# A decoder layer on one core: two more products by quarters, seven instead of eight

## The chip, the cores and the metric

The kernel runs on one NeuronCore of a Trainium2 chip. The metric is the device time of one execution in microseconds; the time before is the median of three runs. A profile is one execution recorded by the hardware profiler. Engines are named as it names them: PE is the matrix engine (PEld its weight loads), DVE the vector engine, ACT the scalar engine, POOL the GpSimd engine, SP the engine that issues most DMAs.

## The reference

One decoder layer on x of 512 tokens and 1024 channels, float32:

```python
h = x @ w_in[i]
ua, va, za, qh, kh, vh, zb, ga, gb = jnp.split(h, IN_OFFSETS, axis=-1)
...
ya = ua * sa.reshape(bn, s_len, A_WIDTH) * jax.nn.silu(za)
...
yb = o.reshape(bn, s_len, B_WIDTH) * jax.nn.silu(zb)
merged = jax.nn.sigmoid(ga) * (ya @ w_branch_a[i]) + jax.nn.sigmoid(gb) * (yb @ w_branch_b[i])
mix_out = merged @ w_out[i]
ple = jax.nn.sigmoid(x @ w_ple_gate[i]) * (p[i] @ w_ple[i])
x = layer_norm(DEEPNORM_ALPHA * x + mix_out + ple, ln_g[i], ln_b[i])
```

Branch A is gated spatial mixing, branch B differential attention. What matters here is the last part: the products `ya @ w_branch_a` (called `wa` in the kernel), `yb @ w_branch_b` (`wb`), `merged @ w_out` (`out`), each 512 x 1024 by 1024 x 1024, and the last norm.

## The kernel before

**Numbers.** PE multiplies rounded halves. Every float32 operand is split into a high part (a copy rounded to float32r, by ACT) and a low part (the rest, a subtraction by DVE), and `three` (L282) issues three products per tile: high by high, high by low, low by high. `cut` does this for activations; for weights `prep` and `spread` do, on tiles of 128x1024 that a DMA brought (`wr`, split into `wh` and `wl`; L400 the copy, L403 the subtraction).

**Order.** The program is written out in one order. `product` (L270) counts PE's products on a clock and runs an agenda: `later(n, fn)` puts a step n products further on. The instructions of each engine stand in the order in which the agenda emits them, each engine works its own queue in that order, and semaphores make it wait for others. An engine's instruction whose operand is late holds up all behind it.

**Two ways to multiply.** `token_chunk` takes a stage in two column halves; each of its 8 weight tiles serves all 4 token tiles, 24 products. `quad` takes the 512 x 1024 operand in quarters (two halves of the tokens, two of the inner channels) and does seven products of quarters instead of eight, 24 products in each of seven steps. It needs sums of quarters on both sides. The sums of the weights are made by DMAs that add to what lies in a tile (`follow`, L375, on POOL's queue) or ready in DRAM; those of activations must be there as further operands (`operands`, L635). The seven results are combined from the PSUM banks: ACT keeps some in SBUF (`keep`, L651), DVE adds or subtracts (`block`, L656), and `done` takes the result on. Two weight tiles serve only 24 products then, and are split one step ahead.

**Stages.** v, va, za, ga, gb, pg and `wb` use `quad`; `wa` and `out` use `token_chunk`, and the last four token tiles of `out`'s second half are written out, the last in two halves of 256 columns. Between, `ple` multiplies the embeddings. ga and gb wait in DRAM and come back as tiles. `mb_done` (L1325) multiplies `wb`'s result by its gate, `merge` (L1348, L1349) multiplies `wa`'s and adds, `merge_turn` transposes the merged tile on PE and splits it, `residue` (L1280) adds alpha x to the embeddings in `base`, `residual` (L1375) adds `out`'s bank and takes the statistics, `last_norm` (L1382, L1386) finishes a token tile and stores it. All of these run on DVE, except the transposes and a power of the variance on POOL (L1181).

## Time and profile before

| what | us |
|---|---|
| median of three runs | 620.74 |
| lowest and highest | 620.26, 621.10 |
| the profiled execution: its span (all that the page gives of its time) | 618.3 |
| of it DVE busy | 458.8 |
| of it ACT busy | 327.3 |
| PE's last product ends, from the span's start | 611.3 |

The span runs from the first to the last instruction. The page names a tile written and the tiles read (`out<-in`), how many, the busy time and the mean of one. A busy time adds up stretches in which at least one instruction ran; matmuls overlap, so their own durations (0.39 us) are longer than the distance of their starts. A row of the timeline gives the start, the duration, the engine, the line and the operation; in brackets stands the idle time of the engine before it and what ended it.

### The profile page before, as it was taken

To read this page: it belongs to the slowest core of one execution; us is meant where nothing else is said; L and a number is where in the kernel's file an instruction comes from. 1 tells how busy PE (TensorE), PEld (TensorE's weight loads), DVE (VectorE), ACT (ScalarE), POOL (GpSimd) and SP (SyncE) were. 2 spreads that over 40 slices of the span, in tenths; PEclk is the share of its full clock that TensorE was granted. 3 is DMA by queue.
4 is the path that set the end of the run, shared out by engine and by line. 5 is a ranking of instruction groups with operands and counts; after the bars stand their busy time and mean duration, and the time that the engine had idled before them with its cause. 6 is when DMAs were issued, how large, how long until landed. Compare 5 with 4: busy or idle time off the path is not lost.

```text
span 618.3 us, 8634 instructions
## 1 busy us (share of the span) xinstructions
PE 610.0 (99%) x3036; PEld 514.3 (83%) x3036; DVE 458.8 (74%) x800; ACT 327.3 (53%) x528; POOL 108.7 (18%) x120
## 2 busy tenths in 40 slices
PE   9999999999999999999999999999999999999995
PEld 6888888888888888888889988888888888888885
DVE  6996587878878866857578887677657659476486
ACT  6655664655645655478656765456567445232200
POOL 1234021332432620230102120111110010000011
PEclk9999999999999999999999999999999999999999
DMA  8689899679798598689898898999978997753002
GB/s 305 220 244 183 263 301 271 230 206 283 250 268 282 182 281 267 156 271 304 272 308 197 228 247 242 223 249 284 270 207 259 354 270 241 235 193 117 1 34 103
DMA packets 49888, 143.78 MB, mean 233 GB/s; under 512 B 6452, under 2 KB 7604, under 8 KB 49524
## 3 DMA queue, kind: packets, MB, share of 16 engines
q1 hardware_dynamic: 38772, 110.05, 50.4%
q0 software_dynamic: 8192, 28.58, 25.7%
q10 hardware_dynamic: 2880, 4.59, 2.0%
q8 instruction: 24, 0.39, 0.3%
q14 instruction: 20, 0.16, 0.1%
HBM read 120.00 MB, written 34.73 MB: 250 GB/s over the span
## 4 chain that ended last, share of the span: by engine, by line
PE 99%; DVE 0%; issue 0%; DVEq 0%
PE ps_pp L271 56%; PE ps_sc L271 18%; PE ps_tx L271 9%; PE ps_sc L821 3%; PE ps_po L866 3%; PE ps_po L271 3%; PE ps_tr L271 3%; PE ps_tr L855 1%; PE ps_po L475 1%; PE ps_tr L1208 1%; PE ps_po L1208 1%; PE ps_tx L905 0%; PE ps_sc L1355 0%; PE ps_pp L1355 0%; DVE base L1386 0%
## 5 line engine op out<-in xcount | busy, mean ns | idle before, releaser
L403 DVE TENSOR_TENSOR wl<-wr,wh 128x1024 fp32r<-128x1024 f32 (+1 forms) x136 | 166.4, 1227 | 53.8 <-ACT wh L400 53.1
L400 ACT ACTIVATE wh<-wr 128x1024 fp32r<-128x1024 f32 (+1 forms) x136 | 139.9, 1033 | 87.1 <-PE ps_po L271 15.6
L271 PE MATMUL ps_pp<-xh,wh 128*128 128x512 f32 (+1 forms) x276 | 109.5, 397 | 0.0
L271 PE MATMUL ps_pp<-xl,wh 128*128 128x512 f32 (+1 forms) x276 | 107.0, 388 | 0.0
L271 PE MATMUL ps_pp<-xh,wl 128*128 128x512 f32 (+1 forms) x276 | 105.4, 382 | 0.0
L834 ACT ACTIVATE p<-p,sth 128x128 f32<-128x128 f32 (+3 forms) x64 | 35.5, 556 | 47.3 <-DVE sth L832 47.2
L271 PEld LDWEIGHTS ps_pp<-xh,wl 128*128 128x128 f32 x276 | 52.0, 189 | 8.7
L271 PEld LDWEIGHTS ps_pp<-xh,wh 128*128 128x128 f32 x276 | 52.2, 189 | 8.4 <-ACT wh L297 0.5
L271 PEld LDWEIGHTS ps_pp<-xl,wh 128*128 128x128 f32 x276 | 52.2, 189 | 8.3 <-DVE xl L298 0.4
L375 POOL DMA_DIRECT2D wr<-in_w x26 | 22.6, 869 | 156.8 <-DVE wl L403 136.8
L828 DVE CUSTOM_DVE_ANT_0 p<-ps_sc,mask 128x128 f32<-128x128 f32 (+3 forms) x64 | 30.9, 483 | 5.6 <-PE ps_sc L821 5.6
L766 POOL TENSOR_TENSOR hl<-m,hl 128x512 fp32r<-128x512 f32 x16 | 25.1, 1609 | 54.7 <-ACT hl L761 54.7
L271 PE MATMUL ps_pp<-wh,xl 128*128 128x512 f32 x84 | 32.9, 391 | 0.0
L271 PE MATMUL ps_pp<-wl,xh 128*128 128x512 f32 x84 | 32.8, 390 | 0.0
L271 PE MATMUL ps_pp<-wh,xh 128*128 128x512 f32 x84 | 32.7, 389 | 0.0
L271 PE MATMUL ps_sc<-wh,xsh 128*128 128x512 f32 x80 | 31.2, 390 | 0.0
L271 PE MATMUL ps_sc<-wl,xsh 128*128 128x512 f32 x80 | 31.1, 389 | 0.0
L271 PE MATMUL ps_sc<-wh,xsl 128*128 128x512 f32 x80 | 31.1, 389 | 0.0
L1181 POOL TENSOR_TENSOR rs<-mv,mhalf 128x1 f32<-128x1 f32 x8 | 7.7, 961 | 121.6 <-DVE mv L1179 121.6
L271 PE MATMUL ps_pp<-wl,xsh 128*128 128x512 f32 x64 | 25.0, 391 | 0.0
L271 PE MATMUL ps_pp<-wh,xsl 128*128 128x512 f32 x64 | 25.0, 391 | 0.0
L271 PE MATMUL ps_pp<-wh,xsh 128*128 128x512 f32 x64 | 25.0, 390 | 0.0
(365 smaller groups left out, 1389.7 us busy)
## 6 DMA issues: line engine op xcount, KB each, us to landing
wr<-in_w SPq DMA_DIRECT2D x83, 512.0 KB, 4.7
wr<-in_w POOLq DMA_DIRECT2D x22, 512.0 KB, 6.1
k<-hl SPq DMA_DIRECT2D x16, 256.0 KB, 5.2
q<-hl SPq DMA_DIRECT2D x16, 256.0 KB, 4.3
ws_va<-in_w POOLq DMA_DIRECT2D x8, 512.0 KB, 10.9
wr<-ws_va SPq DMA_DIRECT2D x8, 512.0 KB, 4.3
wa<-in_w POOLq DMA_DIRECT2D x6, 512.0 KB, 7.3
kx<-hl SPq DMA_DIRECT2D x12, 256.0 KB, 5.8
```

Of the source, the lines that this page charges most:

```text
L271: pe.matmul(ps, s, m, start=start, stop=stop, skip_group_check=read_within)
L375: pool.dma_start(out=raw[u][:, :n], in_=weights(STEPS[FOLLOWS[u]][1], n), accum_op=OP.add)
L400: act.activation(h, raw[u][:, :width(STEPS[u][0])], AF.Copy)
L403: dve.tensor_tensor(out=l, in0=raw[u][:, :width(STEPS[u][0])], in1=h.bitcast(F32), op=OP.subtract)
L475: pe.matmul(idle, zeros[:, :P], zeros, start=True, stop=True)
L766: pool.tensor_tensor(out=hl[:, 3 - j, :], in0=m[2 * j], in1=hl[:, j, :].bitcast(F32), op=OP.subtract)
L821: pe.matmul(sc[m][:, :n], q[:, m, i * P:(i + 1) * P], kk[:, m, :n], start=o == 0, stop=o == 1)
L828: dve.tensor_tensor_reduce(out=pr[m][:, :n], in0=sc[m][:, :n], in1=mask[:, T - n:], scale=-(DK ** -0.5), scalar=3e38, op0=OP.add, op1=OP.m ...
L834: act.activation(pr[m][:, :n], pr[m][:, :n], AF.Exp, bias=st[:, m:m + 1], scale=-1.0, accum_out=st[:, 2 + m:3 + m])
L866: pe.matmul(po[:, i * P:(i + 1) * P], at[:, j * P:(j + 1) * P], v[:, j, h * P:(h + 1) * P], start=j == 0, stop=j == i)
L1181: pool.tensor_tensor(out=rs, in0=mv[:, 1:2], in1=mhalf[:, 0:1], op=OP.pow)
L1208: pe.matmul(sa[:, t * P:(t + 1) * P], va[:, t, g * P:(g + 1) * P], aux[0][:, 0, g, :], start=True, stop=True)
```

## The change

`wa` and `out` become `quad`s (`add` becomes `quad` in `plan`). What they need is added and moved:

- yb's operands (three parts, and four sums read from DRAM) go into the tiles of x's parts, and are issued during `pg`; ya's parts and sums are issued from `ple` on, during `wb`. The sums of ya are made by POOL, in place of ya's quarters.
- The gates of `wb` (six of eight), the residues and the merges (six of eight) move from DVE to POOL; ACT multiplies x by alpha.
- The merged result is transposed; ACT copies it into the place of ua, DVE takes its sums partly straight from the transposed banks, POOL makes two of the differences.
- `out` is added onto `base` piece by piece: ACT's kept banks by POOL, the others by DVE at times that `FOLD` sets.
- The norm of the first two token tiles is divided among ACT, DVE and POOL (`early_norm`); the other two stay with `last_norm`. The seventh step's second token tile is done in two halves of 256 columns.

```diff
+CUTS_YA = (((4, 7), (1, 1), 1, 1), ((76, 7), (0, 0), 0, 0), ((100, 7), (1, 0), 1, 0),
+           ((124, 7), 0, 1, 1), ((148, 7), 2, 1, 0), ((172, 7), 1, 0, 0), ((194, 7), 3, 0, 1))
+SUMS_YA = (((20, 8), (1, 1), OP.subtract, (0, 1), (1, 1)), ((36, 8), (0, 1), OP.subtract, (0, 0), (0, 1)),
+           ((92, 8), (0, 0), OP.subtract, (1, 1), (0, 0)), ((114, 8), (1, 0), OP.add, (0, 0), (1, 0)))
...
+MERGE = (22, 12)
+FOLD = {(0, 0): 56, (1, 0): 20, (1, 1): 1}
+SUMS_OF_M = (2, 8, 20, 36, 54)
-RESIDUE = (32, 24)
+RESIDUE = (44, 20)
...
-    add("wa", "a", token_units(0))
-    add("out", "out", token_units(0))
+    quad("wa", "a", token_units(0))
+    quad("out", "out", token_units(0))
...
         def keep(key, bank):
             kept[key] = tmp[0](key[0])[:, :bank.shape[-1]]
             act.activation(kept[key], bank, AF.Copy)
+            if onto:
+                c, t, op = {"s1": (0, 0, OP.add), "s2": (1, 0, OP.subtract), "s5": (1, 2, OP.add)}[key[0]]
+                z = onto(c, t + key[1])
+                later(3, lambda: pool.tensor_tensor(out=z, in0=z, in1=kept[key], op=op))
...
         def block(c, t, first, second, op, spare):
+            if onto:
+                of_bank = second if first is spare else first
+                later(FOLD[c, t // 2], done, c, t, op if first is spare else OP.add, of_bank)
+                return
...
-        later(20, lambda: dve.scalar_tensor_tensor(out=z, in0=x, scalar=ALPHA, in1=z,
-                                                   op0=OP.mult, op1=OP.add))
+        later(40, lambda: act.activation(x, x, AF.Copy, scale=ALPHA))
+        later(42, lambda: pool.tensor_tensor(out=z, in0=x, in1=z, op=OP.add))
...
+    def add_ya(to, op, x, y, part):
+        pool.tensor_tensor(out=ya_quarter(*to, part), in0=ya_quarter(*x, part), in1=ya_quarter(*y, part), op=op)
...
     def mb_done(c, t, z, source):
-        dve.tensor_tensor(out=z, in0=source, in1=gate.pop(("gb", c, t)), op=OP.mult)
+        engine = pool if source is z else dve
+        engine.tensor_tensor(out=z, in0=source, in1=gate.pop(("gb", c, t)), op=OP.mult)
...
+    def merge(c, t, z, source):
+        dve.tensor_tensor(out=z, in0=source, in1=gate.pop(("ga", c, t)), op=OP.mult)
+        final = (c, t // 2) == (0, 1)
+        engine = dve if final else pool
+        engine.tensor_tensor(out=z, in0=z, in1=mb[0][:, t, c * T:(c + 1) * T], op=OP.add)
+        later(MERGE[final], merge_turn, c, t, z)
...
     def merge_turn(c, t, m):
+        bank = pbank("tr" if t % 2 else "po", 1)
         for j in range(4):
             pe.transpose(bank[:, j * P:(j + 1) * P], m[:, j * P:(j + 1) * P], ident)
         turned = bank.rearrange("p (j t) -> p j t", j=4)
+        if (c, t // 2) != (0, 1):
+            act.activation(raw_of(c, t), turned, AF.Copy)
+            raw = raw_of(c, t)
+            later(2, split_of, {(0, 0): (0, 0), (1, 0): (1, 0), (1, 1): (0, 1)}[c, t // 2], t, raw, 3)
+            if c and t < 2:
+                later(8, lambda: pool.tensor_tensor(out=raw, in0=raw, in1=raw_of(0, t), op=OP.subtract))
+            return
+        m0, m1, m2, m3 = raw_of(1, t), raw_of(0, t - 2), raw_of(1, t - 2), raw_of(0, t)
+        dve.tensor_tensor(out=m0, in0=turned, in1=m0, op=OP.subtract)
+        dve.tensor_tensor(out=m2, in0=m0, in1=m2, op=OP.add)
+        dve.tensor_tensor(out=m3, in0=m1, in1=turned, op=OP.subtract)
+        later(SUMS_OF_M[0], split_of, 0, t, m0, 4)
+        later(SUMS_OF_M[1], lambda: pool.tensor_tensor(out=m1, in0=m0, in1=m1, op=OP.subtract))
+        later(SUMS_OF_M[2], split_of, 2, t, m2, 4)
...
+    def early_norm(t):
+        mv, rs = rstd_of(zst[t])
+        lg, lb = norm_last
+        z = base[:, t, :]
+        mean = small([P, 1], "mean")
+        pool.tensor_scalar(out=mean, in0=mv[:, 0:1], scalar1=-1.0, scalar2=None, op0=OP.mult)
+
+        def centre():
+            act.activation(z, z, AF.Identity, bias=mean[:, 0:1])
+            later(4, lambda: act.activation(z, z, AF.Copy, scale=rs[:, 0:1]))
+            later(8, lambda: dve.tensor_tensor(out=z, in0=z, in1=lg, op=OP.mult))
+            later(10, lambda: pool.tensor_tensor(out=z, in0=z, in1=lb, op=OP.add))
+            later(11, sp.dma_start, out[t * P:(t + 1) * P, :], z)
+
+        later(8, centre)
```

How the rows of three engines change at three places (line numbers of the changed kernel are those of its own file; L413 is the subtraction that was L403, L385 the adding DMA that was L375):

On POOL, from `wb` to the end, all rows before the change were these three:

```order
L375 DMA wr_4685<-in_w 128x1024
L375 DMA wr_4733<-in_w 128x1024
L1181 TENSOR_TENSOR rs<-mv,mhalf 128x1 x4
```

After it, POOL's rows from `ple` to the start of `wa` are these (ua holds ya, L1341 makes its sums, L1367 are the gates of mb, L1323 the residues):

```order
L1341 TENSOR_TENSOR ua<-ua 128x2x256 x4
L1367 TENSOR_TENSOR mb<-mb,two 128x512
L1341 TENSOR_TENSOR ua<-ua 128x2x256
L1367 TENSOR_TENSOR mb<-mb,two 128x512
L1341 TENSOR_TENSOR ua<-ua 128x2x256 x3
L385 DMA wr_4694<-in_w 128x1024
L1323 TENSOR_TENSOR base<-x,base 128x512
L385 DMA wr_4732<-in_w 128x1024
L1323 TENSOR_TENSOR base<-x,base 128x512
L1367 TENSOR_TENSOR mb<-mb,two 128x512 x2
L1323 TENSOR_TENSOR base<-x,base 128x512
L1367 TENSOR_TENSOR mb<-mb,two 128x512
```

The two DMAs that add weights now stand behind and between these.

On DVE, at the passage from `wa` to `out`, the merges of `wa`'s second half and their low parts stood so (gate holds ga and then the merged tile, ml is its low part, L1280 the residue):

```order
L1348 TENSOR_TENSOR gate<-ps_pp,gate 128x512
L1349 TENSOR_TENSOR gate<-gate,mb 128x512
L403 TENSOR_TENSOR wl<-wr_5122,wh 128x1024
L1359 TENSOR_TENSOR ml<-ps_pp,mh 128x4x128
L1348 TENSOR_TENSOR gate<-ps_tx,gate 128x512
L1349 TENSOR_TENSOR gate<-gate,mb 128x512
L1359 TENSOR_TENSOR ml<-ps_pp,mh 128x4x128 x2
L1280 SCALAR_TENSOR_TENSOR base<-x,base 128x512
```

They now stand so (s are kept results of `wa`, two the gates, xl low parts of the merged result, z the last merged tile, L1436 to L1438 the sums from the transposed bank):

```order
L1403 TENSOR_TENSOR s_5239<-s_5239,two 128x512
L413 TENSOR_TENSOR wl<-wr_5025,wh 128x1024
L1421 TENSOR_TENSOR xl<-ua,xh 128x4x128
L413 TENSOR_TENSOR wl<-wr_5103,wh 128x1024
L1403 TENSOR_TENSOR z<-ps_pp,two 128x512
L1406 TENSOR_TENSOR z<-z,mb 128x512
L1421 TENSOR_TENSOR xl<-ua,xh 128x4x128
L1436 TENSOR_TENSOR ua<-ps_po,ua 128x4x128
L1437 TENSOR_TENSOR ua<-ua 128x4x128
L1438 TENSOR_TENSOR ua<-ua,ps_po 128x4x128
```

Two splits of `out`'s weights stand ahead of z, and the sums behind it.

On DVE, the last rows before the last token tile were one tile after another, each five kinds of rows, as here for the third:

```order
L1375 TENSOR_TENSOR base<-ps_pp,base 128x512
L1376 BN_STATS vst<-base 128x6
L1178 BN_AGGR mv<-vst 128x2
L1179 TENSOR_SCALAR mv<-mv 128x1
L1382 SCALAR_TENSOR_TENSOR base<-base,mv,lg 128x1024
L1386 SCALAR_TENSOR_TENSOR base<-base,rs,lb 128x1024
```

Now, behind the split of the last weight tile, additions of several token tiles and the parts of `early_norm` (L1467) stand ahead of the third tile's norm:

```order
L413 TENSOR_TENSOR wl<-wr_5103,wh 128x1024
L1454 TENSOR_TENSOR base<-base,ps_pp 128x512
L1455 BN_STATS vst<-base 128x6
L1454 TENSOR_TENSOR base<-base,ps_sc 128x512
L1455 BN_STATS vst<-base 128x6
L1203 BN_AGGR mv<-vst 128x2
L1204 TENSOR_SCALAR mv<-mv 128x1
L1454 TENSOR_TENSOR base<-base,ps_tx 128x512
L1455 BN_STATS vst<-base 128x6
L1467 TENSOR_TENSOR base<-base,ln_g 128x1024
L1454 TENSOR_TENSOR base<-base,ps_pp 128x512
L1455 BN_STATS vst<-base 128x6
```

The second L1467, of the second token tile, stands behind the third tile's norm and ahead of the last tile.

## The prediction

> **What bounds the kernel now.** The page's table of busy time comes first, then its chain of waits, then the busy time by stage.

> ```profile
> PE 610.0 (99%) x3036; PEld 514.3 (83%) x3036; DVE 458.8 (74%) x800; ACT 327.3 (53%) x528; POOL 108.7 (18%) x120
> PE 99%; DVE 0%; issue 0%; DVEq 0%
> 481.94:520.02 38.08, 38.08 (x169) 31.53 (x168) 26.14 (x32) 19.46 (x23) 1.72 (x2) 1.00 0.91 293
> 520.02:565.40 45.38, 45.38 (x209) 37.60 (x208) 28.76 (x38) 13.38 (x17) 0.00 (x0) 1.00 0.63 215
> 565.40:611.30 45.90, 45.89 (x233) 38.81 (x231) 31.87 (x45) 7.59 (x9) 4.50 (x3) 1.00 0.06 25
> 611.30:618.33 7.03, 0.00 (x0) 0.00 (x0) 3.89 (x8) 0.00 (x0) 0.92 (x1) 0.85 0.37 143
> ```

> The window rows are the stages `wb`, `wa` and `out`, cut where the tiles that PE reads change (ybh, yah, mh), and what follows PE's last product. Columns: stretch, its length, busy time of PE, PEld, DVE, ACT, POOL, granted clock, DMA share, GB/s. PE is busy throughout at full clock, so a product less is time less, as long as no other engine makes PE wait. DVE is busy for about 70% of each stage, POOL hardly at all. After PE stops, 7.03 us remain.

> PE's busy time is a union of overlapping matmuls, so I take the pace from starts: a chain piece of 48 products with 512 columns, and the first and last of the 48 products with 256 columns that end the kernel.

> ```profile
> 492.99 10.88 PE ps_sc L271 x48
> 605.38 0.28 PE L271 MATMUL ps_pp<-wh,mh 128*128 128x256 f32 x1
> 611.01 0.28 PE L271 MATMUL ps_pp<-wh,ml 128*128 128x256 f32 x1
> ```

> 10.88 / 48 = 0.2267 us, and (611.01 - 605.38) / 47 = 0.120 us.

> **PE's own part.** `wa` and `out` take 8 x 4 x 2 x 3 = 192 products each now; 48 of `out` are half as wide and count for 24 full ones. That is 360 full and 48 half products, 81.6 + 5.8 = 87.4 us. By quarters they take 7 x 2 x 4 x 3 = 168 each, 12 of them cut in two: 324 full and 24 half, 73.5 + 2.9 = 76.3 us. The 32 transposes stay. PE falls by **11.0 us**, and the order shows the same 36 full and 24 half matmuls fewer, so that the change might not do what it says is no rival.

> **What DVE and POOL get.** Each of the two stages splits 14 weight tiles instead of 8. DVE keeps that, and POOL takes work that was DVE's or is new: 38 additions or products of 128x512 (8 sums of ya, 6 gates of mb, 8 residues, 6 merges, 4 sums of the merged result, 6 additions onto base) and two of 128x1024. Until now POOL did nothing here for 93 us (the bracket in the first row below). The trace prices what happens when both engines read SBUF:

> ```profile
> 596.64 1.53 POOL L1181 TENSOR_TENSOR rs<-mv,mhalf 128x1 f32<-128x1 f32 x1 [93.08 <-DVE mv L1179]
> 57.90 2.87 POOL L766 TENSOR_TENSOR hl<-m,hl 128x512 fp32r<-128x512 f32 x2
> 59.41 2.44 DVE L403 TENSOR_TENSOR wl<-wr,wh 128x1024 fp32r<-128x1024 f32 x1 [2.37 <-ACT wh L400]
> 494.94 2.35 DVE L403 TENSOR_TENSOR wl<-wr,wh 128x1024 fp32r<-128x1024 f32 x2
> 113.31 2.87 POOL L766 TENSOR_TENSOR hl<-m,hl 128x512 fp32r<-128x512 f32 x2 [17.54 <-ACT hl L761]
> 113.46 1.57 DVE L846 SCALAR_TENSOR_TENSOR p<-p,rho,p 128x384 f32<-128x384 f32 x1
> 114.95 2.31 DVE L403 TENSOR_TENSOR wl<-wr,wh 128x1024 fp32r<-128x1024 f32 x1
> 228.16 0.62 DVE L846 SCALAR_TENSOR_TENSOR p<-p,rho,p 128x384 f32<-128x384 f32 x1
> 187.09 0.68 DVE L828 CUSTOM_DVE_ANT_0 p<-ps_sc,mask 128x512 f32<-128x512 f32 x1
> 186.23 3.35 POOL L766 TENSOR_TENSOR hl<-m,hl 128x512 fp32r<-128x512 f32 x2 [1.81 <-ACT hl L761]
> ```

> Alone, two splits take 2.35 us, one 1.22. Under POOL a split takes 2.44 or 2.31, and the 384-wide operation 1.57 instead of 0.62: the two POOL operations at 113.31 cost DVE (1.57 - 0.62) + (2.31 - 1.22) = 2.04 us, **1.02 us each**, and they took turns with DVE. At 186.23 DVE reads a PSUM bank meanwhile and keeps its 0.68. So a POOL operation costs DVE 1.02 us if it meets a DVE operation with two SBUF operands, and nothing beside one that reads PSUM, or a pause.

> [...]

> DVE's own prices are starts of one operation to the next: 2.35 - 1.22 = 1.13 us for a split of 128x1024, 0.61 us for 128x512 (588.55 - 587.94); an addition with the statistics that wait for it is 589.87 - 588.55 = 1.3. ACT's rows for a weight tile and a bank stand below them:

> ```profile
> 587.94 0.69 DVE L1376 BATCH_NORM_STATS2 vst<-base 128x6 f32<-128x512 f32 x1
> 588.55 0.68 DVE L1375 TENSOR_TENSOR base<-ps_sc,base 128x512 f32<-128x512 f32 x1
> ...
> 589.87 0.67 DVE L1375 TENSOR_TENSOR base<-ps_tr,base 128x512 f32<-128x512 f32 x1
> ...
> L400 ACT ACTIVATE wh<-wr 128x1024 fp32r<-128x1024 f32 x122 | 128.4, 1055 | 85.5 <-PE ps_po L271 15.6 <-PE ps_sc L271 15.4 <-PE ps_tx L271 11.6
> L651 ACT ACTIVATE s<-ps_pp 128x512 f32<-128x512 f32 x19 | 11.3, 595 | 20.2 <-PE ps_pp L271 20.1
> ```

> **First stall, in `wb`.** From the split of the first weight tile of `wb`'s third step to that of the second tile of `wa`'s first step, DVE has 31 operations: 12 splits, 12 low parts of ya, 7 that read PSUM. 12 x 1.13 + 19 x 0.61 = 25.2 us. POOL has 14 of its 38 there: 14.3 us. PE passes from 5 products into `wb`'s second step to 7 into `wa`, 6 x 24 + 2 = 146 products or 33.1 us, of which ACT's first copy takes 1.06: 32.0 are left. Serial, DVE and POOL need 39.5 us; with all seven PSUM operations (4.3 us) beside POOL, 35.2. PE then waits 3.2 to 7.5 us; should DVE lose nothing, 25.2 fits and PE waits 0. I take **5.0**, the middle of the upper pair: most DVE operations there have two SBUF operands.

> **Second stall, from `wa` to `out`.** PE must transpose the last merged tiles (z) before it goes on with `out`, and z's product and addition are the last of 14 DVE operations: from the second block of c = 1 on, 4 splits and 10 operations of 128x512 (4 of these read PSUM), 4.5 + 6.1 = 10.6 us. POOL has 5 of its 38 between (three merges, two differences): 5.1 us. A set of four transposes moves PE's next start by 0.36 us, taken as 0.4:

> ```profile
> 568.58 0.60 PE L1355 MATMUL ps_pp<-ident,gate 128*128 128x128 f32 x4
> 568.94 0.48 PE L271 MATMUL ps_sc<-wh,ml 128*128 128x512 f32 x1
> ```

> From the end of `wa`'s fifth step to z's transpose PE has 48 products and four such sets, 10.9 + 1.6 = 12.5 us, of which ACT's split and copy of a bank (1.06 + 0.60) pass before DVE can begin: 10.8 are left. DVE alone, 10.6, fits; with all five of POOL it needs 15.7. The wait is 0 to 4.9 us, and the second z, one tile later, adds up to 1. I take **4.0**, near the upper end, because ten of the 14 operations have two SBUF operands. Queued behind z on DVE are the sums of the merged result and two splits for `out`, late by the same amount; PE is late by then as well.

> **The end.** Rows of the last two token tiles:

> ```profile
> 605.58 0.69 DVE L1375 TENSOR_TENSOR base<-ps_pp,base 128x512 f32<-128x512 f32 x1 [0.67 <-PE ps_pp L271]
> 607.03 0.21 DVE L1178 BATCH_NORM_AGGREGATE mv<-vst 128x2 f32<-128x12 f32 x1
> 607.34 1.27 DVE L1382 SCALAR_TENSOR_TENSOR base<-base,mv,lg 128x1024 f32<-128x1024 f32 x1
> 610.26 0.42 DVE L1375 TENSOR_TENSOR base<-ps_pp,base 128x256 f32<-128x256 f32 x1
> 613.91 1.41 DVE L1386 SCALAR_TENSOR_TENSOR base<-base,rs,lb 128x512 f32<-128x512 f32 x2
> ```

> A full tile takes DVE 610.26 - 605.58 = 4.7 us, the last one 615.32 - 610.26 = 5.1; DVE ends 615.32 - 611.30 = 4.0 us after PE, and the store adds 3.0. In the changed kernel tiles 2 and 3 both finish in the last step. Before them DVE has, from the last step but one on, behind the split of the last step's first tile: one more split and two products with ln_g (1.13 each), four additions with statistics (1.3 each) and two aggregates (607.34 - 607.03 = 0.3 each), 3.4 + 5.2 + 0.6 = 9.2 us, then 4.7 and 5.1: 19.0 us. PE has those two steps, 36 full and 24 half products or 11.0 us, of which ACT's copy and that first split take 2.2, or up to 1 less if they start early: 8.8 to 9.8. DVE ends 9.2 to 10.2 us after PE, 5.2 to 6.2 more than now. Less than now it cannot be: the last tile's own 5.1 stays, and one tile more stands in front. I take **+5.3**, since ACT is mostly idle there and can start early.

> **At nothing.** The DMA rows that carry this:

> ```profile
> L375 POOL DMA_DIRECT2D wr<-in_w x26 | 22.6, 869 | 156.8 <-DVE wl L403 136.8 <-DMA wr<-ws_pg 16.0 <-DVE ua L1149 1.7
> wr<-in_w POOLq DMA_DIRECT2D x22, 512.0 KB, 6.1
> ```

> Of 28 weight tiles instead of 16, 16 come as accumulations on POOL's queue, behind its additions. They issue in 0.87 us, land 6.1 us later and are needed two steps (10.9 us) on, where the DMA share was 0.63 and 0.06; one POOL operation in front of each still fits, and with more in front each such step would wait about 1 us. ACT's extra copies (12 at 1.06, 12 at 0.60, 8 of x) fit in the 70 us that it is idle in `wa` and `out`. The loads of gates and x that move on SP's queue are covered by the same DMA share. None of this can give time either, since PE waits for none of it now.

> **Sum**, against the profiled span: 618.3 - 11.0 + 5.0 + 4.0 + 5.3 = 621.6. The median of the three runs, 620.74, lies 2.4 above that span; with these 2.4 around it: **624.0 us**, slower.

> **Rivals.**
> *POOL finds DVE's pauses* (ends faster). `wb` has 32.0 - 25.2 = 6.8 us to spare: if fewer than half of the 14 POOL operations (14.3 us) stop DVE, that stall vanishes, and the second shrinks to about 0.2 if the five do likewise. For it: at 186.23 two of them cost nothing. Against: that was beside PSUM reads, 7 of 31 here. 618.3 - 11.0 + 0.2 + 5.3 + 2.4 = 615.2.
> *The end is covered too*: 618.3 - 11.0 + 2.4 = 609.7. Against: the 19.0 us are all DVE's own.
> *The stalls in full*, as where every POOL operation stops DVE: 618.3 - 11.0 + 7.5 + 5.9 + 6.2 + 2.4 = 629.3.
> *Even*: stalls of 5.7 us in all, with the end at 5.3, cancel the gain: 620.7.

> **Chances.** Forecast 0.40 (622 to 628), POOL in the pauses 0.25, end covered too 0.06, stalls in full 0.14, even 0.15. Faster by over 0.2%, which is about what a measurement can tell from no change: 0.25 + 0.06 + 0.02 of even = 0.33; within 0.11; slower 0.40 + 0.14 + 0.02 = 0.56. The range, 614.5 to 629.5, leaves out the covered end, what lies beyond the full stalls and some of the second case. The forecast's own range is 622 to 628.

> **What would show it.** Right: splits (L413 after) of 2.1 us and more in `wb`, beside POOL; idle PE before the splits' first users in `wb` and before z's transposes; DVE ending 9 us or more after PE. PE's sum in `wa` and `out` should fall by 11.0 in any case. Wrong: PE with no idle time and splits of 1.22 us beside a busy POOL, or DVE in step with PE at the end.

## The result, and the profile after

The changed kernel takes **636.11 us** (median of 4 runs, 634.05 to 636.89), the kernel before in the same session 620.55 (620.26 to 621.1): a ratio of 1.0245, with a 95% interval of 1.0227 to 1.0262. It is slower by 15.6 us; forecast were 624.0 and at most 629.5. The profiled execution is the fastest of the four: 634.05 us, span 632.3. From here on "the end" is what follows PE's last product.

The page's busy times and chain of waits, which stood at PE 610.0 and 99% before:

```profile
PE 605.8 (96%) x2976; PEld 505.9 (80%) x2976; DVE 500.8 (79%) x808; ACT 362.8 (57%) x576; POOL 189.8 (30%) x178
PE 81%; DVE 7%; DMA 5%; issue 3%; POOL 2%; ACT 1%; DVEq 0%; ACTq 0%; POOLq 0%
```

60 matmuls are gone, as forecast (36 full, 24 half), but the chain leaves PE for a fifth of the span. Busy time by stage, cut at the first product of `wb`, `wa` and `out` and behind the last (columns as in the prediction):

```profile
481.73:527.10 45.37, 40.84 (x170) 32.40 (x168) 38.66 (x33) 26.17 (x37) 27.47 (x16) 0.96 0.75 244
527.10:570.27 43.17, 41.31 (x189) 33.26 (x188) 36.86 (x33) 24.73 (x33) 24.01 (x19) 1.00 0.83 206
570.27:617.80 47.53, 43.16 (x193) 33.99 (x191) 43.13 (x52) 23.52 (x31) 23.50 (x23) 0.96 0.52 100
617.80:632.33 14.53, 0.00 (x1) 0.00 (x0) 10.53 (x17) 0.84 (x1) 7.12 (x4) 0.67 0.36 144
```

Before, the four were 38.08, 45.38, 45.90 and 7.03 us. By quarters `wa` should lose 24 x 0.2267 = 5.4 us and `out` 12 x 0.2267 + 24 x 0.120 = 5.6. Against 38.1, 39.9, 40.3 and 7.0 the changed kernel is late by 7.3 us in `wb`, 3.2 in `wa`, 7.2 in `out` and 7.5 at the end: 25.2 lost, 11.0 gained. (One set of four transposes has moved from `out` to `wa`, so about 0.4 us of `wa`'s figure belong to `out`; the total stays.) Where PE stood, its rows of the timeline with the idle time in brackets:

```profile
502.62 0.50 PE L281 MATMUL ps_sc<-wl,xsh 128*128 128x512 f32 x1 [2.10 <-DVE wl L413]
520.34 0.47 PE L281 MATMUL ps_pp<-wh,xh 128*128 128x512 f32 x1 [1.10 <-DVE mb L674]
543.57 0.66 PE L1426 MATMUL ps_po<-ident,s 128*128 128x128 f32 x4 [1.31 <-POOL s L1406]
574.41 0.70 PE L1426 MATMUL ps_po<-ident,z 128*128 128x128 f32 x4 [2.79 <-DVE z L1406]
589.28 0.50 PE L281 MATMUL ps_sc<-wl,xsh 128*128 128x512 f32 x1 [1.06 <-DVE wl L413]
```

Two of these waits cost more than their length. The stretches around the first show the granted clock in the column after POOL's:

```profile
500.00:502.00 2.00, 0.52 (x3) 0.10 (x1) 2.00 (x2) 2.00 (x5) 2.00 (x2) 1.00 0.86 297
502.00:504.00 2.00, 1.38 (x4) 1.15 (x5) 2.00 (x2) 1.02 (x2) 1.72 (x1) 0.79 0.53 138
504.00:506.00 2.00, 2.00 (x6) 1.57 (x5) 2.00 (x3) 0.00 (x0) 0.90 (x2) 0.50 0.93 355
```

PE is idle for most of the first row, and in the third, never idle, it starts a product every 0.43 us instead of every 0.23, at a granted clock of 0.50. The same follows the wait for z at 574.41. Each such stretch lasts 3.4 us and holds about 8 products, so it costs 1.6 us on top of the wait.

DVE and POOL just ahead of that first wait, rows of both in order of time:

```profile
491.98 1.66 POOL L1367 TENSOR_TENSOR mb<-mb,two 128x512 f32<-128x512 f32 x1 [11.30 <-DVE mb L674]
492.41 2.31 DVE L413 TENSOR_TENSOR wl<-wr,wh 128x1024 fp32r<-128x1024 f32 x1
493.61 2.27 POOL L1341 TENSOR_TENSOR ua<-ua 128x512 f32<-128x512 f32 x1
496.88 3.48 DVE L1338 TENSOR_TENSOR xl<-ua,xh 128x512 fp32r<-128x512 f32 x2
498.07 5.65 POOL L1341 TENSOR_TENSOR ua<-ua 128x512 f32<-128x512 f32 x3
500.28 4.52 DVE L413 TENSOR_TENSOR wl<-wr,wh 128x1024 fp32r<-128x1024 f32 x2
```

A split takes 2.31 us, two low parts 3.48 instead of 1.29, two splits 4.52 instead of 2.35; POOL's own additions stretch to 2.27. They take turns, one instruction each, and DVE has hardly a pause left in which POOL could work: it is busy for 38.6 of the 40 us from 490 to 530.

### The profile page after: what moved, and what is told of

Same layout as the page of the kernel before. It is cut to its first block, busy times and chain, and to the rows that moved or that the text cites. A ratio compares the mean times of both kernels' runs of the same rounds, so it can differ in the third digit from the quotient of the medians.

```text
span 632.3 us, 8694 instructions
## 1 busy us (share of the span) xinstructions
PE 605.8 (96%) x2976; PEld 505.9 (80%) x2976; DVE 500.8 (79%) x808; ACT 362.8 (57%) x576; POOL 189.8 (30%) x178
## 4 chain that ended last, share of the span: by engine, by line
PE 81%; DVE 7%; DMA 5%; issue 3%; POOL 2%; ACT 1%; DVEq 0%; ACTq 0%; POOLq 0%
PE ps_pp L281 49%; PE ps_sc L281 13%; PE ps_tx L281 7%; DMA wr<-in_w 5%; PE ps_sc L846 3%; PE ps_po L891 3%; DVE wl L413 2%; PE ps_tr L880 1%; PE ps_po L281 1%; PE ps_tr L281 1%; ACT wh L410 1%; DVE xl L1338 1%; PE ps_po L485 1%; PE ps_tr L1233 1%; PE ps_po L1233 1%
## 5 line engine op out<-in xcount | busy, mean ns | idle before, releaser
L413 DVE TENSOR_TENSOR wl<-wr,wh 128x1024 fp32r<-128x1024 f32 (+1 forms) x149 | 194.6, 1311 | 41.3 <-ACT wh L410 38.2
L410 ACT ACTIVATE wh<-wr 128x1024 fp32r<-128x1024 f32 (+1 forms) x149 | 153.6, 1034 | 66.9 <-DMA wr<-in_w 17.7
L385 POOL DMA_DIRECT2D wr<-in_w x42 | 37.0, 881 | 126.6 <-DVE wl L413 100.8
L281 PE MATMUL ps_pp<-wl,xh 128*128 128x512 f32 x136 | 54.4, 400 | 1.5 <-DVE wl L413 1.4
L281 PE MATMUL ps_pp<-wh,xh 128*128 128x512 f32 x136 | 53.8, 395 | 1.2 <-DVE mb L674 1.1
L281 PE MATMUL ps_pp<-wh,xl 128*128 128x512 f32 x136 | 53.8, 396 | 0.0
L281 PE MATMUL ps_sc<-wl,xsh 128*128 128x512 f32 x112 | 44.9, 401 | 3.6 <-DVE wl L413 3.6
L281 PE MATMUL ps_sc<-wh,xsh 128*128 128x512 f32 x112 | 44.4, 397 | 0.0
L281 PE MATMUL ps_sc<-wh,xsl 128*128 128x512 f32 x112 | 44.2, 395 | 0.0
L281 PEld LDWEIGHTS ps_pp<-wl,xh 128*128 128x128 f32 x136 | 25.9, 191 | 7.9 <-DVE wl L413 2.7
## 6 DMA issues: line engine op xcount, KB each, us to landing
wr<-in_w SPq DMA_DIRECT2D x79, 512.0 KB, 5.2
wr<-in_w POOLq DMA_DIRECT2D x38, 512.0 KB, 6.3
ws_va<-in_w POOLq DMA_DIRECT2D x8, 512.0 KB, 10.0
wr<-ws_va SPq DMA_DIRECT2D x8, 512.0 KB, 4.4
wa<-in_w POOLq DMA_DIRECT2D x6, 512.0 KB, 7.8
```

Of the source, the lines that this page charges most:

```text
L281: pe.matmul(ps, s, m, start=start, stop=stop, skip_group_check=read_within)
L385: pool.dma_start(out=raw[u][:, :n], in_=weights(STEPS[FOLLOWS[u]][1], n), accum_op=OP.add)
L410: act.activation(h, raw[u][:, :width(STEPS[u][0])], AF.Copy)
L413: dve.tensor_tensor(out=l, in0=raw[u][:, :width(STEPS[u][0])], in1=h.bitcast(F32), op=OP.subtract)
```

## The experiments

Three theories stood at the start. **L** (lock): a POOL operation stops a DVE operation that reads two SBUF tiles, as the prediction priced it (1.02 us each). **S** (saturation): POOL costs DVE nothing, and DVE is simply full. **W** (weights): the adding DMAs of the weights come late, behind POOL's additions. The times of the kernels, with the lengths of the stages cut as above:

| kernel | median, us | wb | wa | out | end |
|---|---|---|---|---|---|
| before | 620.5 | 38.08 | 45.38 | 45.90 | 7.03 |
| changed | 636.11 | 45.37 | 43.17 | 47.53 | 14.53 |
| x1, all additions on DVE | 626.66 | 40.10 | 41.37 | 45.90 | 14.67 |
| x3, only those of ple and wb on DVE | 626.08 | 39.96 | 40.89 | 47.18 | 14.25 |
| x2, POOL's additions left out | 617.96 | 38.71 | 41.46 | 42.01 | 12.14 |
| x4, drain late | 637.28 | 45.35 | 42.91 | 48.38 | 16.91 |
| x5, x1 with z later | 625.38 | 39.99 | 40.99 | 46.27 | 14.66 |
| x6, x1 without two norms | 621.91 | 39.72 | 42.07 | 46.10 | 9.86 |
| y5, only wa by quarters | 620.07 | 39.97 | 40.96 | 47.32 | 7.81 |
| y6, y5 with moves | 623.94 | 39.47 | 41.48 | 50.47 | 7.74 |
| y7, y6 with alpha x on POOL | 625.02 | 39.14 | 45.26 | 48.26 | 7.76 |
| y8, another order of out | 622.88 | 39.56 | 46.12 | 45.42 | 7.77 |
| y9, y8 with alpha x early | 618.38 | 40.05 | 41.31 | 45.42 | 7.84 |

### x1: POOL's additions on DVE

```diff
-        pool.tensor_tensor(out=ya_quarter(*to, part), ...)
+        dve.tensor_tensor(out=ya_quarter(*to, part), ...)
...
-        engine = pool if source is z else dve
+        engine = dve
```

and so for every line with `pool.tensor_tensor` from `ple` on.

> Every addition or product of 128x512 (and the two of 128x1024) that the changed kernel gives to POOL from ple to the end goes to DVE instead, 38 + 2 operations; nothing else changes. Theory L (lock: a POOL operation stops a DVE operation that reads two SBUF tiles): in the changed kernel DVE's rows from 471 us on are together about 30 us longer than the shortest of their shape, 0.75 us for each POOL operation. On DVE they cost 38 x 0.61 + 2 x 1.13 = 25.5 us. So DVE gains about 4.5 us, splits return to 1.22 us, and the time falls slightly: 627 to 636 us, 632 likeliest. Rival S (POOL's work runs beside DVE's, and DVE is simply full with 28 splits and the new low parts): DVE gets 25 us more where it is busy already, and the time rises to 645 us or more. Rival W (the adding weight DMAs come late because they queue behind POOL's additions): POOL's queue is free, so the time falls too, to 626 to 632, with ACT's copies no longer waiting for DMA.

626.66 us (625.57 to 628.0), ratio 1.0107 (1.009 to 1.0124): 9.5 us less than the changed kernel although DVE has 40 operations more. S, which forecast 645 or more, is out. The time lies just under L's range (627 to 636) and inside W's, so the rows must tell these two apart. Groups of DVE's rows by shape between 482 and 545 us, of the changed kernel:

```profile
L413 DVE TENSOR_TENSOR wl<-wr,wh 128x1024 fp32r<-128x1024 f32 x18 | 30.6, 1718 | 8.2 <-ACT wh L410 6.9 <-PE ps_pp L281 1.3
L1338 DVE TENSOR_TENSOR xsl<-ua,xsh 128x512 fp32r<-128x512 f32 x8 | 10.1, 1276 | 0.0
L1338 DVE TENSOR_TENSOR xl<-ua,xh 128x512 fp32r<-128x512 f32 x4 | 4.8, 1230 | 0.0
L1403 DVE TENSOR_TENSOR s<-s,four 128x512 f32<-128x512 f32 x2 | 3.7, 1836 | 0.1
```

and of x1:

```profile
L413 DVE TENSOR_TENSOR wl<-wr,wh 128x1024 fp32r<-128x1024 f32 x21 | 25.5, 1223 | 7.9 <-ACT wh L410 7.7
L1338 DVE TENSOR_TENSOR xsl<-ua,xsh 128x512 fp32r<-128x512 f32 x8 | 5.5, 689 | 0.0
L1338 DVE TENSOR_TENSOR xl<-ua,xh 128x512 fp32r<-128x512 f32 x4 | 2.7, 685 | 0.0
L1403 DVE TENSOR_TENSOR s<-s,four 128x512 f32<-128x512 f32 x2 | 1.4, 688 | 0.0
```

The means (the number behind the busy time, ns) fall back to 1223 and 690. The excess in the changed kernel is 18 x 0.495 + 8 x 0.587 + 4 x 0.545 + 2 x 1.148 = 18.1 us, over the 19 POOL additions that start in this stretch 0.95 us each. On DVE one costs 0.61. Where DVE had no pause, handing an addition to POOL cost DVE one and a half times what doing it cost. POOL's additions were held up too: one of 128x512 lasted 2.27 us in the rows at 493.61, and 1.27 at 542.25.

### x3: only the part of ple and wb

`SUMS_YA`, the gates of mb and alpha x on DVE (three of the lines of x1), merges and the rest on POOL.

> Only the 22 POOL operations of ple, wb and the start of wa (8 sums of ya, 6 gates of mb, 8 additions of alpha x) go to DVE; the merges and what is added in out stay on POOL. L: DVE's excess in 471 to 543 us, about 20 us, is replaced by 22 x 0.61 = 13.4 us; the stalls in wb and at the start of wa, 7.6 us with the half clock, shrink to 2 to 5; the rest stays: 629 to 634 us. S: 13 us more on a full DVE: 643 or more.

626.08 us (624.92 to 627.12), better than forecast (629 to 634). `wb` falls from 45.37 to 39.96 us and `wa` from 43.17 to 40.89, although `wa`'s merges are still POOL's, so most of the loss of both was POOL's work in `ple`, `wb` and the start of `wa`. In `out`, x1, which has the merges and the sums on DVE too, is better by 1.3 us; PE waited 2.5 us for the first z here and 1.5 for the second.

### x2: POOL's additions left out

The same lines as in x1, removed.

> The same 40 POOL operations are left out altogether (the sums of ya, six gates of mb, alpha x, six merge additions, the differences of the merged result, the kept banks and ln_b are missing from what is computed). This prices all of POOL's work in the changed kernel. L: PE's stalls of 17.5 us in all (10.5 us of waits, two stretches at half clock worth 3.4, the rest around them) shrink to 0 to 4, and DVE's end comes about 1 to 3 us nearer to PE's: 616 to 622 us, 618 likeliest. S: DVE's own 28 splits and low parts are still there, the stalls stay for the most part: 628 to 636. W: like L here, POOL's queue being free; the two part in the adding DMAs: under W their issue comes earlier by more than a microsecond each against the split ahead of them, under L the splits themselves come earlier.

617.96 us (617.76 to 618.26), ratio 0.996 (0.9945 to 0.9975), as L expected. Its stages:

```profile
481.63:520.34 38.71, 38.51 (x170) 31.37 (x169) 26.90 (x33) 26.17 (x37) 2.59 (x3) 1.00 0.87 287
520.34:561.80 41.46, 40.81 (x190) 33.41 (x189) 29.40 (x35) 24.84 (x33) 7.79 (x9) 1.00 0.90 221
561.80:603.81 42.01, 40.49 (x193) 33.08 (x191) 35.94 (x49) 24.25 (x31) 6.72 (x10) 1.00 0.56 111
603.81:615.95 12.14, 0.00 (x0) 0.00 (x0) 8.52 (x15) 0.00 (x0) 2.39 (x2) 0.69 0.39 157
```

Two things follow. PE's stalls, 7.3 + 3.2 + 7.2 = 17.7 us in the changed kernel, are 2.0 + 1.4 + 5.6 = 9.0 with the same work on DVE and 0.6 + 1.5 + 1.7 = 3.8 without it: half of them goes when POOL's work becomes DVE's, nearly a third is the additions as such. The rest remains with none of them there; what share of it is the 28 splits, the low parts or their order was not separated. And even with POOL's work free of charge the end stays 5.1 us longer than before.

W is not borne out: an adding DMA is issued on average 0.55 us after the split ahead of it ends in the changed kernel and 0.31 in x1, at most 1.1 and 0.6 (its row's start less the end of the last split, 18 issues each), where W asked for more than a microsecond each. And ACT waits about as long for the weights without POOL's additions (13.9 us in x1). Waits by releaser, 482 to 611 us, us and times, of the changed kernel:

```profile
ACT wh L410 <- DMA wr<-in_w: 15.5, 9, 3.5
```

of x2, with none of these additions on POOL:

```profile
ACT wh L410 <- DMA wr<-in_w: 19.8, 12, 3.2
```

### x4: POOL's drain later

```diff
-RETIRE = 126
+RETIRE = 164
```

> POOL's drain, which stands at 607.23 to 613.18 us in the changed kernel and ahead of the first token tile's power of the variance, comes 38 products later, behind the powers and means of tiles 0 and 1; no arithmetic changes. If the drain holds up the early norm: the first power starts at about 609.8 instead of 613.26, DVE's wait of 1.1 us before its product with ln_g goes, and DVE ends about 1 us sooner: 634.5 to 635.5 us. If the drain only waits beside other work: 636. If it then stands in the way of the later norms, slower, up to 639.

637.28 us (636.02 to 637.7), not faster: the first and the third of the mechanisms named there are both real. In the changed kernel the first power waits behind the drain:

```profile
607.26 1.85 POOL L665 TENSOR_TENSOR base<-base,s 128x512 f32<-128x512 f32 x1 [0.63 <-ACT s L661]
613.26 0.56 POOL L1206 TENSOR_TENSOR rs<-mv,mhalf 128x1 f32<-128x1 f32 x1 [4.15 <-DVE base L1454]
```

In x4 the first power starts at 611.02, right behind its mean and variance (610.95), and DVE's wait of 1.1 us before the product with ln_g is gone. Now it is the last power that waits, and DVE waits for it, the last step of all:

```profile
630.63 0.55 POOL L1206 TENSOR_TENSOR rs<-mv,mhalf 128x1 f32<-128x1 f32 x1 [4.15 <-issue]
631.21 1.42 DVE L1482 SCALAR_TENSOR_TENSOR base<-base,rs,ln_b 128x512 f32<-128x512 f32 x2 [3.52 <-POOL rs L1206]
```

In both kernels the drain holds POOL for 4.15 us behind the operation ahead of it (607.26 + 1.85 to 613.26 in the first pair). The time of x4 does not price the drain alone: behind its wait for z it ran 6.8 us at half clock instead of 3.4.

### x5 and x6: z, and the end

x5 is x1 with `MERGE = (22, 24)`.

> x1 (all of POOL's additions on DVE, 626.7 us) with one number changed: the last merged tiles z go to their transposes 24 products behind their merge instead of 12. In x1 PE waits 2.4 us for the first z and 0.3 for the second, and then runs 3.4 us at half clock, worth 1.7. If PE only comes to z too early, 12 products (2.7 us) of other work cover the wait and the clock stays up: 622 to 624.5 us. If DVE is behind at that place altogether, the wait moves to the sums and splits that stand behind z, and the time stays at 625 to 628.

625.38 us (623.94 to 626.01), in the range of the second case. The wait at z is gone, but PE then waits 1.9 and 0.8 us for splits of `out` at 577.75 and 580.70 us, and runs 6.8 us at half clock there. DVE was behind at this place altogether.

x6 is x1 without the two operations of `early_norm` on DVE:

```diff
-            later(8, lambda: dve.tensor_tensor(out=z, in0=z, in1=lg, op=OP.mult))
-            later(10, lambda: dve.tensor_tensor(out=z, in0=z, in1=lb, op=OP.add))
```

> x1 (626.7 us) without the products with ln_g and additions of ln_b for the first two token tiles, which are missing from what is computed: four DVE operations of 128x1024, 1.23 us each, all between PE's last two steps and the last token tile. In x1 DVE ends 11.7 us behind PE. If the end is DVE's own serial work from the last split on, DVE ends 4 x 1.23 = 4.9 us sooner: 621.8 us (620.8 to 622.8). If the chain of the early norm on ACT, POOL's powers or the stores set the end, less than 2 us goes: 625 to 627.

621.91 us (620.43 to 624.37), and the end shrinks from 14.67 to 9.86 us, by 4.8: it is DVE's serial work, as the prediction had it.

### p1: the additions alone, in the kernel before

```diff
-        later(20, lambda: dve.scalar_tensor_tensor(out=z, in0=x, scalar=ALPHA, in1=z,
-                                                   op0=OP.mult, op1=OP.add))
+        later(20, lambda: act.activation(x, x, AF.Copy, scale=ALPHA))
+        later(22, lambda: pool.tensor_tensor(out=z, in0=x, in1=z, op=OP.add))
...
-        dve.tensor_tensor(out=m, in0=m, in1=mb[0][:, t, c * T:(c + 1) * T], op=OP.add)
+        pool.tensor_tensor(out=m, in0=m, in1=mb[0][:, t, c * T:(c + 1) * T], op=OP.add)
```

> The kernel before with one part of the change alone: its 8 additions of alpha x (ACT multiplies by alpha) and its 8 additions in the merges, all 128x512 with both operands in SBUF, go from DVE to POOL; nothing is by quarters. L: where they meet a DVE operation with two SBUF operands, splits take up to 2.3 us instead of 1.22, about 0.75 us for each POOL operation, 12 us in all for 16 that DVE did in 16 x 0.61 = 9.8; but PE is not late, since the splits have a lead of 8 to 15 us: 620 to 622 us. If POOL ran beside DVE for nothing, splits would stay at 1.22 us, and the time would be the same: the rows tell them apart, not the time. If one late merge already held up the transposes: 623 or more.

620.52 us (620.34 to 621.16), ratio 0.9999 (0.999 to 1.0009). The time is what both cases expected, and by the rows the rival was right here, not L: DVE and POOL in order of time,

```profile
532.53 1.23 DVE L403 TENSOR_TENSOR wl<-wr,wh 128x1024 fp32r<-128x1024 f32 x1 [2.44 <-ACT wh L400]
533.10 1.80 POOL L1281 TENSOR_TENSOR base<-x,base 128x512 f32<-128x512 f32 x1 [29.21 <-ACT x L1280]
545.79 3.78 POOL L1349 TENSOR_TENSOR gate<-gate,mb 128x512 f32<-128x512 f32 x3
546.57 0.69 DVE L1359 TENSOR_TENSOR ml<-ps_sc,mh 128x512 fp32r<-128x512 f32 x1 [1.88 <-ACT mh L1358]
548.46 0.69 DVE L1359 TENSOR_TENSOR ml<-ps_sc,mh 128x512 fp32r<-128x512 f32 x1 [0.60 <-ACT mh L1358]
```

Here POOL waits 0.5 us for a split (1.80 us, where three additions together take 3.78) and then works in DVE's pause, or beside reads of PSUM, which keep their 0.69. Splits take 1.33 us at most. The price of a POOL addition was that of the place: nothing where DVE paused, 0.95 us where it did not.

### y5 to y9: only wa by quarters

`wa` stays a `quad`, `out` becomes `token_chunk` again with the norms of before; the merged tiles go straight into operands, without sums, and all additions to DVE.

```diff
-    quad("out", "out", token_units(0))
+    add("out", "out", [("t", c * T, kk) for c in range(2) for kk in (2, 3, 0, 1)])
```

> Only wa by quarters, out as in the kernel before (two column halves, the last four token tiles one after another, last norm as before), with channels 512 to 1023 of the merged result multiplied first, since they are merged first; all additions on DVE. PE saves 24 products of 0.2267 us, 5.4 us. The end is that of the kernel before (7.0 us behind PE). If what the whole change lost lies in POOL's lock, the sums of the merged result and the end, this keeps most of the 5.4: stalls of 1 to 3 us in wb and at the start of wa as in x3 (1.5), 616 to 619 us, faster than before. If already the 14 splits of wa with a lead of 5 us, or ya's sums, cost as much as they save: 620 to 624.

620.07 us (619.72 to 621.89), ratio 0.9999 (0.9991 to 1.0008): no gain, in the range of the expectation's second case. `wb` and `wa` are as in x3, 1.9 and 1.0 us above what PE needs, and `out` takes 1.4 us more than before; PE waited 1.25 us for z there. y6 moves alpha x (`RESIDUE = (180, 24)`) and z (`MERGE = (22, 28)`):

> The version with only wa by quarters (620.07 us, PE's excess between starts 4.3 us against 0.6 before) with two moves: the eight additions of alpha x, 0.69 us each on DVE, come 136 products later and 24 apart, so that they leave the stretch of 490 to 530 us in which DVE has no pause, and the last merged tiles are transposed 28 products behind their merge, not 12. If DVE's full stretch and the z wait are what eats the 5.4 us: the waits of 1.3 us at z and most of the 2.2 us in wb and at the start of wa go: 617.5 us (616.5 to 618.7), faster than before. If the work moved only shifts the waits: 619.5 to 620.5.

623.94 us (622.93 to 625.5), a miss, above both ranges. `wb` is 0.5 us shorter, but in `out` the wait came back larger, at the first product of token tile 2, and 3.4 us at half clock followed:

```profile
568.18 0.80 PE L281 MATMUL ps_tr<-wh,xh 128*128 128x512 f32 x1 [3.20 <-DVE xl L1418]
```

On DVE three splits, an addition of alpha x and the two steps of the first z stood just ahead of that low part; in y5 the wait for z had covered it.

y7 gives alpha x to POOL in y6:

> As y6, but the eight additions of alpha x are POOL's, with ACT's product before them. They now come where DVE has pauses. In the kernel before such additions on POOL cost DVE nothing (splits at 1.33 us at most, 620.5 us). If POOL is free in pauses: within 0.7 us of y6, or up to 1 us faster. If the lock costs wherever POOL works: 8 x 0.4 us more on DVE, 1 to 3 us slower than y6.

625.02 us (624.61 to 625.73), 1.1 slower than y6, in the range of the lock; but that the lock did it is not shown. `wa` takes 3.8 us more than in y6, and about 2 of these are lost at three waits from 534 to 539 us, ahead of POOL's first addition there (542.23): the weights came late, and DVE stood idle for them. Only one split was held up for long beside an addition, at 556.07: it took 2.16 us instead of 1.22, and PE then waited 1.2 us for a result that stood behind it on DVE.

y8 and y9 begin `out` with two weight tiles together, one token tile after another:

```diff
+    two = next_pair("out", 0)
+    for t in range(NT):
+        for i, k in enumerate(ORDER[:4]):
+            h, l = two[i // 2]
...
-MERGE = (22, 12)
+MERGE = (22, 34)
```

and split `out`'s next two tiles at 14 and 26 products (`SPLITS`). y8 adds alpha x in `wa` (`RESIDUE = (150, 16)`), y9 where y5 does (`(44, 20)`).

> Only wa by quarters, all additions on DVE, and out's first column half begins with the two weight tiles of channels 512 to 1023 taken together, one token tile after another, so that the token tiles 2 and 3 of these channels are wanted 24 products later than in y6, where PE waited 3.4 us for them, and the last merged tiles 60 products into out (transposed 34 behind their merge). The splits of out's next two tiles come at 14 and 26 products of that stretch, behind the merges, and alpha x is added from 520 us on. If the order on DVE at the passage from wa to out is what cost y5 1.3 us and y6 3.4: stalls of 1 to 2.5 us in all are left of the 5.4 that PE saves, 616 to 618.5 us, faster than before. If DVE's late merges only push the wait to the next user: 619.5 to 622.

622.88 us (621.77 to 623.26), above both ranges. `out` is 45.42 us now, 1.9 less than in y5, but `wa` takes 46.12.

> y8 with alpha x added where y5 adds it (from 503 us on, in wb), and nothing else. y8 lost 5 waits of about 1 us each in wa, every one at the first user of a split that came late: in wa a tile's next weights are added by a DMA (6 us) only after the tile's split. If the additions of alpha x in wa made those splits late, they go, the waits of y5 in wb and at the start of wa (2.2 us) come back, and the wait of 1.3 us for z stays away: 618 to 619.3 us, faster than before by 0.2 to 0.4%. If the new order of out itself is what costs: 621.5 to 623.5, as y8.

**618.38 us** (617.58 to 619.39), ratio 0.9964 (0.995 to 0.9978): as expected, and faster than both kernels. PE's waits in `wa`, in y8 and then in y9:

```profile
PE ps_pp L281 <- DVE s L674: 1.7, 2, 0.9
PE ps_pp L281 <- ACT s L661: 0.9, 1, 0.9
PE ps_po L1413 <- DVE s L1406: 0.9, 1, 0.9
PE ps_sc L281 <- DVE wl L413: 0.8, 1, 0.8
```

```profile
PE ps_pp L281 <- DVE wl L413: 0.2, 1, 0.2
```

Only one of y8's five waits is at a split (the last row); the others are for kept, combined or merged results. Eight additions of 0.69 us and their loads, moved out of `wa`, gave 4.8 us there. Whether the additions on DVE or the loads of x, which stand among the weights' loads on SP's queue, did the harm was not separated. For the first two waits (535.58 and 538.11 us) the traces lean to the loads: the first two adding DMAs of `wa` landed 8.2 and 9.4 us after their issue in y8 and 5.3 and 6.2 in y9, DVE was busy for only 3.8 of the 10 us from 525 to 535 in y8, and y7, with none of these additions on DVE, has waits at the same place. But y6, which loads x in `wa` too, has next to none there, so the cause stays open.

## Why the prediction was wrong

The direction was right, and so was the mechanism it priced (POOL's operations stop DVE, by 0.95 us each between 482 and 545 us, PE waits for DVE, and DVE ends late); the time fell 6.6 us outside the range. What failed is what had no price: the places under "At nothing" (5.7 us), the half clock behind two waits (3.2 us), and POOL's part of the end (2.2 us). By its steps:

- **PE's own part**, -11.0: right, 60 matmuls fewer of the forecast kinds.
- **First stall, in `wb`**, forecast 5.0 with bounds of 3.2 and 7.5 (their middle is 5.35): 7.3. Of these 1.6 are the half clock behind the wait, which no term had. The waits themselves come to 5.7, not far above the forecast, at 0.95 us for each POOL addition where 1.02 was assumed.
- **Second stall, at z**, forecast 4.0 with bounds of 0 and 5.9: 2.8 for the first z, 0.3 ahead of it, 1.6 at half clock, 4.7 together. The waits alone, 3.1, are less than forecast: both terms together were 9.0, their waits are 8.8, and the excess is the half clock.
- **The end**, forecast +5.3 with bounds of 5.2 and 6.2: +7.5. It is DVE's serial work, as forecast (x6), and without POOL's work it is +5.1 (x2), so DVE's own sum was right. Nothing was put down for POOL there: `early_norm`'s two additions of ln_b stop DVE too (rows of 1.84 us at 619.35 and 1.68 at 626.03, where x1 has 1.27 and 1.40), and DVE waits 1.1 us for the norm that the drain held up.

```profile
616.45 1.23 DVE L1467 TENSOR_TENSOR base<-base,ln_g 128x1024 f32<-128x1024 f32 x1 [1.12 <-ACT base L1466]
619.35 1.84 DVE L1478 SCALAR_TENSOR_TENSOR base<-base,mv,ln_g 128x1024 f32<-128x1024 f32 x1
627.63 1.40 DVE L1482 SCALAR_TENSOR_TENSOR base<-base,rs,ln_b 128x512 f32<-128x512 f32 x2
```

The second row took 1.27 in the kernel before; the third ends at 629.03, 11.2 us behind PE, where 9.2 to 10.2 were forecast.

- **"At nothing"** is the step that failed outright. What remains of `wa` (3.2 us) and of `out` (7.2 - 4.7 = 2.5) lies at places that the prediction costed at nothing: PE waiting for the first merged tiles, whose addition is POOL's (1.31 us at 543.57), and for splits in `wa` (0.51 at 529.35) and in `out`'s third step (1.06 us at 589.28). These waits make 2.9 of the 5.7; the rest is spread over the two stages, and no single wait shows it. The prediction looked only at whether the DMAs land in time, and not at what POOL's work does to DVE and PE between the two places that it priced. In x3, with the additions of `ple` and `wb` on DVE, the wait for the first merged tiles is gone, though their addition is still POOL's, and the one in `out`'s third step stays (1.04 us); in x1, with the rest on DVE too, that one is gone as well.
- The runs lie further above their spans than the 2.4 us that were carried over: the median, 636.11, lies 3.8 above the profiled span, and the three other executions have spans of 634.1 to 635.2.

Together: 2.3 in `wb`, 0.7 at z, 2.2 at the end, 5.7 at nothing and 1.4 from the runs make 12.3, of 12.1 that the forecast fell short. Of the rivals "stalls in full" (629.3) came closest; POOL finding DVE's pauses, held at 0.25, would have needed the pauses of p1, and DVE had 1.4 us of them in the 40 from 490 to 530.

## What to carry to other kernels

POOL, nearly idle in these stages before, was no spare capacity beside DVE: ask whether the busy engine pauses where the work is put. Where DVE did, POOL's work was free (p1, ratio 0.9999); where it did not, an addition moved away cost DVE 0.95 us against 0.61 for keeping it, and taking POOL's work back made the kernel 9.5 us faster. What PE saved by quarters, DVE paid in the same stage: here `wa` alone could be thinned with a small gain (618.38 us) once alpha x was loaded and added ahead of the stage with late weights, while `out` by quarters lost its 5.6 us to an end that was 5.1 us longer even with POOL's work left out.

## What the runs showed of the hardware

```profile
566.18 0.63 PE L1426 MATMUL ps_po<-ident,z 128*128 128x128 f32 x4 [2.51 <-DVE z L1406]
```

- The length of the wait does not tell these apart; how many products PE started does, in these three runs. In the changed kernel the slow stretches begin at 503.16, 574.84 and, behind PE's end, 622.62, that is 71.68 and 47.78 us apart, 21 and 14 times 3.413. If PE's starts are counted in steps of that length, laid out from these times (a set of four transposes as one, a product of 256 columns as half), a step at full pace holds 15. The steps just ahead of 503.16 and 574.84 hold 4 and 2; of the others from 480 us to PE's last product none holds fewer than 7. The step ahead of the slow stretch in x5 holds 5; in x3 two steps share the wait, the one with fewer products holds 6, and no half clock follows. So a wait cost 1.6 us more where it left 5 products or fewer in a step; why that is so was not shown.
- A drain of POOL's queue held POOL for 4.15 us behind its last operation, also when its last DMA had been issued over 20 us before (x4). Right behind a DMA it lasted longer: its row, 5.9 us in the changed kernel, takes 10.8 us in the kernel before (from 502.67, where POOL has nothing else to do) and 11.1 in x1.
